# Two tiles and GpSimd's DMA queue for side loads, c broadcast by TensorE, and half of a projection in unsplit fp32

## The chip, the cores and the metric

The kernel runs on one core of a Trainium2 chip. The metric is the time of one execution on the device in microseconds; lower is better. TensorE (PE) multiplies matrices out of SBUF into PSUM, VectorE (DVE) and ScalarE (ACT) work element by element, SyncE (SP) issues DMAs here, and GpSimd (POOL) is nearly idle.

## The reference

A decoder trunk of two layers over 256 tokens of width 1024, in fp32. Each layer has a token mixer (layer 0: a short gated convolution; layer 1: differential attention) and then a PEER expert mixer. Each of the four sub-layers takes shift, scale and gate from a vector c:

```python
m = silu(c) @ ada_w[i, s] + ada_b[i, s]         # 1024 x 3072: shift, scale - 1, gate - 1
h = x * (1 + scale) + shift
f = mixer(h)
x = layer_norm(ALPHA * x + (1 + gate) * f, ln_g[i, s], ln_b[i, s])

# the conv mixer
gb, gc, xv = split(h @ w_in, 3); y = gb * conv3(gc * xv); f = y @ w_out
# PEER: the 16 best of 128 x 128 product keys for each of 8 heads and each token
f = sum over the chosen experts of softmax(score) * gelu(h . u[expert]) * v[expert]
```

## The kernel before

**Precision.** A product of fp32 operands is made of three products of split operands. `split` (L92) makes a high part by an ACT copy (L87) and a low part by a DVE subtraction (L90); `mm3` (L140 to L143) and its copies in `project_out` (L352) and `V_steps` (L874) add high x high, high x low and low x high. Small products of attention (L517, L551) and transposes (L207) use fp32 as it is.

**Tiles.** Weights come in tiles of 128 x 1024 fp32, 512 KB, by SP's queue. `raw` (L76) hands out such tiles from a ring of 6 (`STREAM`), in turn with a second ring while a token mixer has one (12 in conv, 4 in attention). `spt` (L80) hands out split tiles from a ring of 10 (`SPBUFS`). In the conv mixer SP issues in program order (`Sync`, L65); after it the scheduler sets the order.

**Order.** Each mixer yields steps, each with a first half (load and split) and a second half (multiply), and `pipeline` (L104) runs the first halves three steps ahead of the second. The framework's scheduler then fixes the order on each engine from its own estimate of times; each engine works through its queue in that order and waits where something is missing.

**The ada columns.** shift, scale and gate are sums over rows of `ada_w` times silu(c). One column (`ada_column`, L173) is one 512 KB load and one DVE pass with accumulation against `csb`, silu(c) on all partitions (L177). There are 96: 16 set the first h of the conv mixer (`h_first`, `h_second`), 24 more fill the conv mixer, 48 the first expert layer and 8 the second. These fills are generators (`ada_unit`, L179: eight columns, two for each `yield`, and a sum) that `advance` (L324) moves on between steps; in the projection of the conv mixer they are held behind the last y (`behind`, L227).

**The conv mixer** (L358). x comes as one DMA of 1 MB behind the first four ada columns. h is made by four pairs of columns of x; `half_second` multiplies the first half of `conv_w_in` as h comes, `project_step` (L305) the second half; `use` (L364) makes y, split into `yh` and `yl`; `project_out` (L338) multiplies by `conv_w_out` in four steps q of two rows of weights k.

**Norm** (L235). Behind each mixer: gate times the accumulators (L266), plus ALPHA times X (L268), square sums on ACT (L270), scaling (L286), then transposes and splits of the next h (`make_hT`, L200). ln's gain and bias are put on X later (`affine`, L292, its DVE passes in L297), out of the way.

**The expert layer** (L646). The query products, then `topk`, then three chunks of the 128 rows of keys (46, 42, 40): U products with Gelu into a ring, gate matrices (`G_step`: DVE makes one-hot factors in L825 to L829, PE multiplies them in L838, DVE multiplies the ring in L840), V products (L874). U of the third chunk and V of the first alternate; V of the third chunk, `vs(2)`, comes last and needs all gates of its chunk.

Of the kernel before, what the change touches and what calls it, by code (L numbers as in the profile page):

```python
# [11 lines left out]
F32 = mybir.dt.float32  # L12
# [16 lines left out]
PH = 8  # L29
# [8 lines left out]
SPBUFS = 10  # L38
STREAM = 6
# [4 lines left out]
def tile_trunk(ctx: ExitStack, tc: tile.TileContext, x, c, columns, ada_w, ln_g, ln_b, conv_w_in_a, conv_w_in_b,  # L44
# [103 lines left out]
    nc.sync.dma_start(csb, rows_bcast(c[0], D))  # L148
    X = const.tile([P, NT, D], F32, name="X")

# [14 lines left out]
    act.activation(csb, csb, AF.Silu)  # L165
# [7 lines left out]
    def ada_column(i, s, part, n, dst):  # L173

        w = raw()
        sync.dma_start(w, ada_w[i, s, part, n])
        return lambda: dve.scalar_tensor_tensor(w, w, 1.0, csb, op0=ALU.mult, op1=ALU.mult, accum_out=dst)  # L177

    def ada_unit(i, s, part):  # L179
        a = small.tile([P, KC], F32, tag="ada", name="ada", bufs=2)  # L180
        for q in range(KC // 2):
            for f in [ada_column(i, s, part, n, a[:, n:n + 1]) for n in (2 * q, 2 * q + 1)]:
                f()
            yield
        at = slice(None), 2 * i + s, slice(KC * part, KC * part + KC)
        dve.tensor_tensor(mod[at], a, ada_bT[at], op=ALU.add)
        yield
# [47 lines left out]
    class Norm:  # L235
# [102 lines left out]
    def project_out(w, yT, accs, engs):  # L338
        def first(q):
            return [load(w[(2 * q + kk) * P:(2 * q + kk + 1) * P, :], engs[kk]) for kk in range(2)]  # L340

        def second(q, parts):
            if q == 0:
                accs.extend(new_accs())
            yh, yl = yT[q]
            for t in range(NT):
                rows = slice(t * P, (t + 1) * P)
                for kk, (wh, wl) in enumerate(parts):
                    k = 2 * q + kk
                    for lhs, rhs, first, last in ((yh, wh, True, False), (yh, wl, False, False), (yl, wh, False, True)):  # L350
# [7 lines left out]
    def conv_mixer(j, hT, cp, fill, prep):  # L358
        gbT = [None] * KC
        gcT = [None] * KC  # L360
        yh = cp.tile([P, KC, T], F32R, name="yh")
        yl = cp.tile([P, KC, T], F32R, name="yl")

        def use(n, ps):  # L364
# [9 lines left out]
            y = cp.tile([P, T], F32, tag="y", name="y", bufs=2)  # L374
# [642 lines left out]
```

## Time and profile before

| what | value |
|---|---|
| median of 3 runs | 1955.66 us (1955.38 to 1959.54) |
| profiled execution | 1956.54 us, its span 1954.8 us |
| PE busy | 1885.1 us, 96% of the span |
| DVE busy | 1550.6 us, 79% |
| ACT busy | 905.3 us, 46% |
| POOL busy | 9.5 us |
| data moved | 378.87 MB, mean 194 GB/s |

The span is that of the instructions on the core, 1.7 us less than the execution. Busy time of PE is the time in which some matmul was under way, also where it ran at a lower clock. A chain of waits on a page names what released each instruction; the views below give the instructions themselves.

### The profile page before, as it was taken

The page shows a single profiled execution, that of the slowest core. Times are in us where ns is not written, and L with a number is a line of the kernel's source. Part 1 is how long each engine was busy: PE and PEld are TensorE (multiplying, and loading weights), DVE is VectorE, ACT ScalarE, POOL GpSimd, SP SyncE. Part 2 cuts the span into 40 slices and gives each one's busy share as a digit, 9 for nine tenths or more (in the row PEclk, how much of TensorE's full clock was granted, in tenths as well). Part 3 has the DMA queues.
Part 4 walks back from the last instruction along what each step waited for, and adds up shares of the span by engine and source line. Part 5 has one row for each costly group of instructions (what it writes and reads, how often), then busy time and mean ns, then how long its engine had stood idle before and what let it go on. Part 6 is the DMA issues. An engine that isn't in the chain of part 4 may idle for free.

```text
span 1954.8 us, 36946 instructions
## 1 busy us (share of the span) xinstructions
PE 1885.1 (96%) x14858; PEld 1720.6 (88%) x14858; DVE 1550.6 (79%) x3138; ACT 905.3 (46%) x1191; POOL 9.5 (0%) x28
## 2 busy tenths in 40 slices
PE   7969999999999999989899899999999999999897
PEld 6969999999999988867798799999999999888786
DVE  7989887887888888876677788878878766888755
ACT  4534555334444444434466545653444444444443
POOL 0000000000000000000100000000000000000000
PEclk9989999999999999999999999999999999999999
DMA  9955655556778765568753246555567555555563
GB/s 383 366 187 159 185 180 177 163 158 210 249 243 256 232 201 173 173 198 279 241 182 111 86 152 184 183 174 161 161 208 226 173 175 181 168 169 181 173 194 97
DMA packets 104412, 378.87 MB, mean 194 GB/s; under 512 B 11568, under 2 KB 12208, under 8 KB 104240
## 3 DMA queue, kind: packets, MB, share of 16 engines
q1 hardware_dynamic: 104096, 376.42, 59.8%
q8 instruction: 116, 1.90, 0.4%
q14 instruction: 56, 0.46, 0.1%
q10 hardware_dynamic: 144, 0.09, 0.0%
HBM read 375.42 MB, written 1.05 MB: 193 GB/s over the span
## 4 chain that ended last, share of the span: by engine, by line
PE 91%; DVE 5%; DMA 2%; issue 1%; ACT 1%; SPq 0%; DVEq 0%; ACTq 0%
PE acc L874 34%; PE ps L141 15%; PE ps L142 15%; PE ps L143 15%; PE ps L838 4%; DVE raw L177 2%; PE acc L352 2%; PE acc L142 2%; PE acc L141 2%; PE acc L143 2%; DVE spt L90 1%; DMA raw<-in_ada_w 1%; DMA X<-in_x 1%; PE ps L517 0%; DMA gsub<-in_attn_subln_g 0%
## 5 line engine op out<-in xcount | busy, mean ns | idle before, releaser
L87 ACT ACTIVATE spt<-raw 128x1024 fp32r<-128x1024 f32 x608 | 641.1, 1058 | 745.3 <-PE ps L142 416.5
L90 DVE TENSOR_TENSOR spt<-raw,spt 128x1024 fp32r<-128x1024 f32 x608 | 741.0, 1222 | 171.3 <-ACT spt L87 166.5
L141 PE MATMUL ps<-hh,spt 128*128 128x256 f32 x2400 | 684.9, 286 | 2.9 <-DVE hh L214 2.4
L142 PE MATMUL ps<-hl,spt 128*128 128x256 f32 x2400 | 681.0, 284 | 0.6 <-DVE hl L90 0.6
L143 PE MATMUL ps<-hh,spt 128*128 128x256 f32 x2400 | 680.5, 284 | 0.0
L874 PE MATMUL acc<-spt,wh 128*128 128x512 f32 x2048 | 565.9, 396 | 4.4 <-ACT wh L87 4.4
L141 PEld LDWEIGHTS ps<-hh,spt 128*128 128x128 f32 x2400 | 460.6, 192 | 6.8 <-issue 3.0
L142 PEld LDWEIGHTS ps<-hl,spt 128*128 128x128 f32 x2400 | 461.4, 192 | 4.0 <-DVE hl L90 0.9
L143 PEld LDWEIGHTS ps<-hh,spt 128*128 128x128 f32 x2400 | 461.3, 192 | 0.0
L874 PEld LDWEIGHTS acc<-spt,wh 128*128 128x128 f32 x2048 | 375.9, 188 | 75.8 <-ACT wh L87 4.6
L874 PE MATMUL acc<-spt,wl 128*128 128x512 f32 x1024 | 319.6, 392 | 3.6 <-DVE wl L90 3.6
L874 PEld LDWEIGHTS acc<-spt,wl 128*128 128x128 f32 x1024 | 191.9, 188 | 44.8 <-DVE wl L90 5.1
L177 DVE SCALAR_TENSOR_TENSOR raw<-raw,csb 128x1024 f32<-128x1024 f32 x96 | 116.1, 1223 | 57.8 <-DMA raw<-in_ada_w 57.7
L87 ACT ACTIVATE wh<-ring 128x512 fp32r<-128x512 f32 x128 | 79.9, 627 | 159.0 <-PE acc L874 148.9
L840 DVE SCALAR_TENSOR_TENSOR ring<-ps,ring 128x368 f32<-128x368 f32 (+2 forms) x192 | 98.1, 512 | 68.6 <-PE ps L838 68.0
L825 DVE TENSOR_TENSOR A<-iota_e,jT 128x1024 f16<-128x1024 f16 x192 | 131.0, 683 | 0.0
L829 DVE TENSOR_TENSOR B<-B,gT 128x368 f16<-128x368 f16 (+2 forms) x384 | 125.1, 334 | 4.0
L90 DVE TENSOR_TENSOR wl<-ring,wh 128x512 fp32r<-128x512 f32 x128 | 88.0, 689 | 38.7 <-ACT wh L87 38.2
L838 PEld LDWEIGHTS <-A 128*128 128x128 f16 x3072 | 91.0, 96 | 31.1 <-issue 14.3
L838 PE MATMUL ps<-B,A 128*128 128x46 f16 (+2 forms) x3072 | 111.7, 182 | 6.6 <-DVE B L829 6.6
L805 ACT ACTIVATE ring<-ps 128x512 f32<-128x512 f32 x128 | 74.7, 584 | 33.8 <-PE ps L143 33.7
L827 DVE TENSOR_TENSOR B<-iota_e,iT 128x368 f16<-128x368 f16 (+2 forms) x192 | 63.4, 331 | 0.0
(204 smaller groups left out, 1179.9 us busy)
## 6 DMA issues: line engine op xcount, KB each, us to landing
raw<-in_peer_u SPq DMA_DIRECT2D x256, 512.0 KB, 3.8
raw<-in_peer_v SPq DMA_DIRECT2D x256, 512.0 KB, 3.9
raw<-in_ada_w SPq DMA_DIRECT2D x96, 512.0 KB, 4.7
raw<-in_peer_w_q SPq DMA_DIRECT2D x32, 512.0 KB, 4.1
raw<-in_attn_w_qk SPq DMA_DIRECT2D x16, 512.0 KB, 4.4
raw<-in_conv_w_in_a SPq DMA_DIRECT2D x12, 512.0 KB, 10.2
raw<-in_conv_w_in_b SPq DMA_DIRECT2D x12, 512.0 KB, 10.2
raw<-in_conv_w_out SPq DMA_DIRECT2D x8, 512.0 KB, 7.2
```

Source lines behind the costliest of these rows:

```text
L87: act.activation(o, i, AF.Copy, scale=scale)
L90: return eng.tensor_tensor(o, a, b, op=ALU.subtract)
L141: pe.matmul(ps, ah, bh, start=first, stop=False)
L142: pe.matmul(ps, ah, bl, start=False, stop=False)
L143: pe.matmul(ps, al, bh, start=False, stop=last)
L177: return lambda: dve.scalar_tensor_tensor(w, w, 1.0, csb, op0=ALU.mult, op1=ALU.mult, accum_out=dst)
L805: act.activation(ring[:, s:s + 2, :].rearrange("p j t -> p (j t)"), st["ps"], AF.Gelu)
L825: dve.tensor_tensor(by_two(A), numbers(0, KEYS), pairs(jT, KEYS), op=ALU.is_equal)
L829: dve.tensor_tensor(by_two(B[:, h]), by_two(B[:, 1]), pairs(gT[:, h], n), op=ALU.mult)
L838: pe.matmul(ps[:, t, :], A[:, t, :], B[:, h, t, :], start=h == 0, stop=h == 1)
L840: dve.scalar_tensor_tensor(r, ps.rearrange("p t j -> p j t"), 1.0 / GSCALE, r, op0=ALU.mult, op1=ALU.mult)
L874: pe.matmul(acc[t][hf], lhs[:, jj, rows], rhs[:, hf * 512:(hf + 1) * 512], start=first and jp == 0 and jj == 0, stop=last and last_pair an ...
```

## The change

- **Start.** c comes as one row of 4 KB on ACT's queue. TensorE multiplies it by a row of ones, two fp32 products of 512 columns, and ACT takes Silu from PSUM into `csb`. x comes in four quarters of 256 columns, the first on ACT's queue at the start, the others on SP's with the ada columns of their pair.
- **Side loads.** Two tiles of their own (`side`) and GpSimd's queue serve the 48 and 8 ada columns of the expert layers and the gain and bias rows of `affine` there. `ada_units` loads one column ahead and moves on one column for each `yield`. `STREAM` goes from 6 to 5, `SPBUFS` from 10 to 9.
- **Places.** conv: 2 columns for each of six groups of steps and 4 behind each projection step, in place of 2 and up to 4. Expert layers: a column in two of three steps; `affine` moves from step 6 of `vs(2)` to the steps 30, 33 and 35.
- **Projection.** The rows k = 4 to 7 of `conv_w_out` and of y are not split: one fp32 product in place of three.
- **topk** takes its scratch from unused rows of the ring in place of four split tiles.

```diff
-SPBUFS = 10
-STREAM = 6
+SPBUFS = 9
+STREAM = 5
...
     csb = const.tile([P, D], F32, name="csb")
-    nc.sync.dma_start(csb, rows_bcast(c[0], D))
+    crow = raw()[0:1, :]
+    act.dma_start(crow, c)
     X = const.tile([P, NT, D], F32, name="X")
+    def load_x(q):
+        cols = slice(q * 256, (q + 1) * 256)
+        (sync if q else act).dma_start(X[:, :, cols], x[0][:, cols].rearrange("(t p) d -> p t d", p=P))
+    load_x(0)
...
-    act.activation(csb, csb, AF.Silu)
+    ones = wk.tile([1, P], F32, tag="B", name="ones")
+    pool.memset(ones, 1.0)
+    for hf in range(2):
+        ps, cols = bank(), slice(hf * 512, (hf + 1) * 512)
+        pe.matmul(ps, ones, crow[:, cols], start=True, stop=True)
+        act.activation(csb[:, cols], ps, AF.Silu)
...
-    def ada_column(i, s, part, n, dst):
-        w = raw()
-        sync.dma_start(w, ada_w[i, s, part, n])
+    def side():
+        return stream.tile([P, D], F32, tag="side", name="side", bufs=2)
+    def ada_column(i, s, part, n, dst, tile=raw):
+        w = tile()
+        (sync if tile is raw else pool).dma_start(w, ada_w[i, s, part, n])
         return lambda: dve.scalar_tensor_tensor(w, w, 1.0, csb, op0=ALU.mult, op1=ALU.mult, accum_out=dst)
-    def ada_unit(i, s, part):
-        a = small.tile([P, KC], F32, tag="ada", name="ada", bufs=2)
-        for q in range(KC // 2):
-            for f in [ada_column(i, s, part, n, a[:, n:n + 1]) for n in (2 * q, 2 * q + 1)]:
-                f()
-            yield
...
+    def ada_units(*which, tile=raw):
+        def compute(at, a, f, final):
+            f()
+            if final:
+                dve.tensor_tensor(mod[at], a, ada_bT[at], op=ALU.add)
+        loaded = None
+        for i, s, part in which:
...
+            for n in range(KC):
+                f = ada_column(i, s, part, n, a[:, n:n + 1], tile)
+                if loaded:
+                    compute(*loaded)
+                    yield
+                loaded = at, a, f, n == KC - 1
+        compute(*loaded)
         yield
...
-    def ln_params(i, s):
-        gb = raw(), raw()
-        sync.dma_start(gb[0], rows_bcast(ln_g[i, s], D))
-        sync.dma_start(gb[1], rows_bcast(ln_b[i, s], D))
+    def ln_params(i, s, tile=raw):
+        gb = tile(), tile()
+        queue = sync if tile is raw else pool
+        queue.dma_start(gb[0], rows_bcast(ln_g[i, s], D))
+        queue.dma_start(gb[1], rows_bcast(ln_b[i, s], D))
...
-        def affine(self, _):
-            gb = ln_params(self.i, self.s)
+        def affine(self, tile=raw):
+            gb = ln_params(self.i, self.s, tile)
+            yield
             for t in range(NT):
                 for n, op in enumerate((ALU.mult, ALU.add)):
                     dve.tensor_tensor(X[:, t, :], X[:, t, :], gb[n], op=op)
+                yield
...
-    def project_out(w, yT, accs, engs):
+    def project_out(w, yT, accs, engs, whole=KC):
         def first(q):
...
+                if q >= whole:
+                    parts.append((raw(),))
+                    sync.dma_start(parts[-1][0], rows)
+                else:
+                    parts.append(load(rows, engs[kk]))
...
+                    if q >= whole:
+                        products = (yT[q][0], ws[0], True, True),
+                    else:
+                        (yh, yl), (wh, wl) = yT[q], ws
+                        products = (yh, wh, True, False), (yh, wl, False, False), (yl, wh, False, True)
...
-            dve.tensor_tensor(y, y, gbT[k], op=ALU.mult)
+            last["y"] = dve.tensor_tensor(y, y, gbT[k], op=ALU.mult)
+            if k >= half:
+                return
             copy(yh[:, k, :], y)
-            last["y"] = sub(dve, yl[:, k, :], y, yh[:, k, :].bitcast(F32))
+            sub(dve, yl[:, k, :], y, yh[:, k, :].bitcast(F32))
...
-            if q == 0:
-                sync.dma_start(X, x[0].rearrange("(t p) d -> p t d", p=P))
+            if q:
+                load_x(q)
...
-                    yield advance(fill)
+                    yield advance(fill, 2)
...
-            for st in project_out(conv_w_out[j], yT, acc, SUBS):
+            for st in project_out(conv_w_out[j], yT, acc, SUBS, 2):
                 yield st
-                yield advance(fill, 2, ("hT", "y"))
+                yield advance(fill, 4, ("hT", "y"))
...
-                    yield None, late
+                    yield drain(late())
...
+        cand = scratch(PH * NCAND).rearrange("p (h k) -> p h k", **hk)
+        f = scratch(6 * P).rearrange("p (n k) -> p n k", n=6)
+        eq, keys = (scratch(1024).bitcast(F16).rearrange("p (h k a) -> p h k a", h=PH, k=TOPK) for _ in range(2))
...
-                if n % 2 == 1:
+                if n % 3 != 0:
                     yield advance(fill)
...
+            rest = late(side)
             for n, v in enumerate(vs(2)):
                 yield v
-                if n % 3 == 2:
+                if n % 3 != 0 and n < n2 - 10:
                     yield advance(fill)
-                if n == 6:
-                    yield None, late
+                if n == n2 - 10:
+                    yield drain(fill)
+                    yield advance(rest)
                 if n == n2 - 8:
-                    yield drain(fill)
                     yield None, prep
+                if n in (n2 - 7, n2 - 5):
+                    yield advance(rest)
...
-        fill = units((0, 0, 2), (0, 1, 0), (0, 1, 1))
+        fill = ada_units((0, 0, 2), (0, 1, 0), (0, 1, 1))
...
-    fill = units((0, 1, 2), (1, 0, 0), (1, 0, 1), (1, 0, 2), (1, 1, 0), (1, 1, 1))
+    fill = ada_units((0, 1, 2), (1, 0, 0), (1, 0, 1), (1, 0, 2), (1, 1, 0), (1, 1, 1), tile=side)
...
-        acc = peer(1, hT, pp, units((1, 1, 2)), norm.prepare, late)
+        acc = peer(1, hT, pp, ada_units((1, 1, 2), tile=side), norm.prepare, late)
```

## Rows read from the trace of the kernel before

**Rows 1.** Page, busy tenths of TensorE in 40 slices of the span
```profile
PE   7969999999999999989899899999999999999897
```

**Rows 2.** Table by stretches: engines' busy us (instructions), PEclk, DMA share, GB/s
```profile
60.00:80.00 20.00, 20.00 (x169) 20.00 (x168) 19.99 (x36) 10.20 (x18) 0.40 (x4) 1.00 1.03 408
...
455.00:701.00 246.00, 246.00 (x1987) 225.14 (x1986) 201.90 (x328) 107.62 (x123) 0.00 (x0) 1.00 0.76 244
...
1435.00:1680.00 245.00, 245.00 (x1979) 224.15 (x1977) 177.63 (x274) 106.91 (x123) 0.00 (x0) 1.00 0.62 194
```

**Rows 3.** In order of time to 17 us: start, duration, engine, line, operation
```profile
2.04 1.86 PE L415 MATMUL acc<-iota_a,zero 128*128 128x512 f16 x4 [2.04 <-POOL z L372]
...
6.96 1.23 DVE L177 SCALAR_TENSOR_TENSOR raw<-raw,csb 128x1024 f32<-128x1024 f32 x1 [1.07 <-DMA raw<-in_ada_w]
...
13.30 1.97 PE L207 MATMUL ps<-ident,X 128*128 128x128 f32 x8 [9.39 <-DMA X<-in_x]
14.46 1.02 ACT L213 ACTIVATE h<-ps,mod 128x256 f32<-128x256 f32 x2 [6.36 <-PE ps L207]
...
16.99 0.39 PE L422 MATMUL acc<-hh,spt 128*128 128x256 f32 x1 [0.24 <-ACT hh L87]
```

**Rows 4.** The same view, TensorE, from the conv mixer into the first expert layer
```profile
113.44 0.62 PE L352 MATMUL acc<-spt,yl 128*128 128x512 f32 x2
...
132.58 0.77 PE L141 MATMUL ps<-hh,spt 128*128 128x256 f32 x2 [1.35 <-DVE hh L214]
```

**Rows 5.** The same view, TensorE, from attention into the second expert layer
```profile
1099.98 0.63 PE L352 MATMUL acc<-spt,yl 128*128 128x512 f32 x2
...
1110.09 0.36 PE L141 MATMUL ps<-hh,spt 128*128 128x256 f32 x1 [1.05 <-DVE hh L214]
```

**Rows 6.** The same view, VectorE, 102 to 123 us
```profile
102.18 1.22 DVE L90 TENSOR_TENSOR spt<-raw,spt 128x1024 fp32r<-128x1024 f32 x1 [0.62 <-ACT spt L87]
103.33 0.75 DVE L90 TENSOR_TENSOR yl<-y,yh 128x256 fp32r<-128x256 f32 x2
104.00 1.22 DVE L177 SCALAR_TENSOR_TENSOR raw<-raw,csb 128x1024 f32<-128x1024 f32 x1
...
122.50 1.23 DVE L268 SCALAR_TENSOR_TENSOR spt<-X,spt 128x1024 f32<-128x1024 f32 x1
```

**Rows 7.** The same view, all engines, end of the first layer's gates
```profile
847.81 0.61 PE L874 MATMUL acc<-spt,wl 128*128 128x512 f32 x2
...
856.03 1.23 DVE L177 SCALAR_TENSOR_TENSOR raw<-raw,csb 128x1024 f32<-128x1024 f32 x1 [0.93 <-DMA raw<-in_ada_w]
...
858.84 3.25 PE L874 MATMUL acc<-spt,wh 128*128 128x512 f32 x8 [3.03 <-ACT wh L87]
```

**Rows 8.** The same view, TensorE, end of the second layer's gates
```profile
1826.83 0.61 PE L874 MATMUL acc<-spt,wl 128*128 128x512 f32 x2
...
1833.27 2.11 PE L874 MATMUL acc<-spt,wh 128*128 128x512 f32 x8 [1.32 <-ACT wh L87]
1836.57 0.73 PE L874 MATMUL acc<-spt,wl 128*128 128x512 f32 x2 [1.20 <-DVE wl L90]
```

**Rows 9.** The same view, TensorE, last V product of each expert layer
```profile
972.25 0.39 PE L874 MATMUL acc<-spt,wl 128*128 128x512 f32 x1
...
1943.49 0.39 PE L874 MATMUL acc<-spt,wl 128*128 128x512 f32 x1
```

**Rows 10.** Who waited for whom, 860 to 960 us: total us, times, longest
```profile
DVE raw L177 <- DMA raw<-in_ada_w: 18.9, 8, 3.5
```

**Rows 11.** DMA issues: destination, source, queue, count, KB each, median us to landing
```profile
raw<-in_ada_w SPq DMA_DIRECT2D x96, 512.0 KB, 4.7
...
out_x<-spt SPq DMA_DIRECT2D x4, 256.0 KB, 2.1
```

**Rows 12.** The same view, TensorE: split and fp32 products
```profile
99.97 1.09 PE L352 MATMUL acc<-spt,yh 128*128 128x512 f32 x4
...
1022.09 1.05 PE L551 MATMUL ps<-v,aT 128*128 128x128 f32 x8
```

More of the change, by code (lines that the diff above doesn't have):

```diff
@@ L171, in tile_trunk @@
     mod = const.tile([P, 4, 24], F32, name="mod")
-    def ada_column(i, s, part, n, dst):
-        w = raw()
-        sync.dma_start(w, ada_w[i, s, part, n])
-        return lambda: dve.scalar_tensor_tensor(w, w, 1.0, csb, op0=ALU.mult, op1=ALU.mult, accum_out=dst)
-    def ada_unit(i, s, part):
-        a = small.tile([P, KC], F32, tag="ada", name="ada", bufs=2)
-        for q in range(KC // 2):
-            for f in [ada_column(i, s, part, n, a[:, n:n + 1]) for n in (2 * q, 2 * q + 1)]:
-                f()
-            yield
-        at = slice(None), 2 * i + s, slice(KC * part, KC * part + KC)
-        dve.tensor_tensor(mod[at], a, ada_bT[at], op=ALU.add)
+    def side():
[3 more added lines that the diff above has]
+        (sync if tile is raw else pool).dma_start(w, ada_w[i, s, part, n])
+        return lambda: dve.scalar_tensor_tensor(w, w, 1.0, csb, op0=ALU.mult, op1=ALU.mult, accum_out=dst)
+    def ada_units(*which, tile=raw):
[5 more added lines that the diff above has]
+        for i, s, part in which:
+            a = small.tile([P, KC], F32, tag="ada", name="ada", bufs=3)
+            at = slice(None), 2 * i + s, slice(KC * part, KC * part + KC)
+            for n in range(KC):
[5 more added lines that the diff above has]
+        compute(*loaded)
         yield
@@ L336, in drain @@
         return None, second
-    def project_out(w, yT, accs, engs):
+    def project_out(w, yT, accs, engs, whole=KC):
         def first(q):
-            return [load(w[(2 * q + kk) * P:(2 * q + kk + 1) * P, :], engs[kk]) for kk in range(2)]
+            parts = []
+            for kk in range(2):
+                rows = w[(2 * q + kk) * P:(2 * q + kk + 1) * P, :]
+                if q >= whole:
[3 more added lines that the diff above has]
+                    parts.append(load(rows, engs[kk]))
+            return parts
         def second(q, parts):
@@ L344, in second @@
                 accs.extend(new_accs())
-            yh, yl = yT[q]
             for t in range(NT):
                 rows = slice(t * P, (t + 1) * P)
-                for kk, (wh, wl) in enumerate(parts):
+                for kk, ws in enumerate(parts):
                     k = 2 * q + kk
-                    for lhs, rhs, first, last in ((yh, wh, True, False), (yh, wl, False, False), (yl, wh, False, True)):
+                    if q >= whole:
[3 more added lines that the diff above has]
+                        products = (yh, wh, True, False), (yh, wl, False, False), (yl, wh, False, True)
+                    for lhs, rhs, first, last in products:
                         for hf in range(2):
@@ L360, in conv_mixer @@
         gcT = [None] * KC
-        yh = cp.tile([P, KC, T], F32R, name="yh")
-        yl = cp.tile([P, KC, T], F32R, name="yl")
+        yh = cp.tile([P, KC // 2, T], F32R, name="yh")
+        yl = cp.tile([P, KC // 2, T], F32R, name="yl")
+        yf = cp.tile([P, KC // 2, T], F32, name="yf")
         def use(n, ps):
@@ L373, in use @@
             dve.tensor_tensor(z[:, 2:], ps, gcT[k], op=ALU.mult)
-            y = cp.tile([P, T], F32, tag="y", name="y", bufs=2)
+            half = KC // 2
+            y = yf[:, k - half, :] if k >= half else cp.tile([P, T], F32, tag="y", name="y", bufs=2)
             col = lambda w: smT[:, 160 + 8 * w + k:161 + 8 * w + k]
@@ L445, in steps @@
                         yield project_step(conv_w_in_b[j, m, 2 * n + b - 4], blk, hT, use, bank, SUBS[b])
[L446 removed]
+                    yield advance(fill, 2)
             yield None, prep
[L448 to L449 removed]
+            yT = [(yh[:, 2 * q:2 * q + 2], yl[:, 2 * q:2 * q + 2]) for q in range(2)]
+            yT += [(yf[:, 2 * q:2 * q + 2],) for q in range(2)]
+            for st in project_out(conv_w_out[j], yT, acc, SUBS, 2):
                 yield st
[L451 removed]
+                yield advance(fill, 4, ("hT", "y"))
             yield drain(fill, ("hT", "y"))
@@ L716, in topk @@
             s0, s1 = sv4[:, :, 0, :], sv4[:, :, 1, :]
-            cand = sp.tile([P, PH, NCAND], F32, tag="sp", name="cand")
             dve.tensor_tensor(cand[:, :, 0:16], s0[:, :, 0:1].to_broadcast([P, PH, 16]), s1, op=ALU.add)
@@ L739, in topk @@
             yield
-            f = sp.tile([P, 6, P], F32, tag="sp", name="f")
             pos = po.rearrange("t h k -> t (h k)")
```

7 lines of the change are left out of this document (removed).

## The prediction

> **What bounds the kernel now.** I first read the page's slices [rows 1]: TensorE (PE) is at nine tenths or more nearly everywhere. So time can only be won where PE stands still, or by giving it less to multiply. The table by stretches [rows 2] says the same by stage: in 60 to 80 us PE is busy for all 20.00 us, VectorE (DVE) for 19.99, the granted clock is 1.00, and the DMA engines move 408 GB/s at a share of 1.03; in the stretches 455 to 701 and 1435 to 1680 us, the same program part of the first and second expert layer, PE is busy for every microsecond of 246 and 245, though the first holds 32 columns of ada weights and the second 8. Work that is taken off DVE, or off the SP queue, in such stretches is worth nothing.
>
> The PE holes, then. (a) The start: the first real matmul begins at 16.99, behind x, for which PE's transposes wait until 13.30 [rows 3]. (b) From the conv mixer to the first expert layer: PE ends its output projection at 114.06 (113.44 + 0.62) and begins the next at 132.58, 18.5 us later [rows 4]. The same passage from attention to the second expert layer runs from 1100.61 to 1110.09, 9.5 us [rows 5]. The difference is DVE: it does 14 ada columns between 104.00 and 122.50, one row like the other, and the norm's L268 begins only then [rows 6]. (c) In the first expert layer, where the last gates meet the last V chunk, PE multiplies no V from 848.42 to 858.84, 10.4 us; in the second layer the same place runs from 1827.44 to 1833.27, 5.8 us, with a last hole of 1.20 at 1836.57 [rows 7, 8]. (d) Behind (c) more is lost in the first layer: from the end of the row at 847.81 to the end of its V products at 972.64 it takes 124.2 us, in the second layer 1827.44 to 1943.88, 116.4 [rows 7, 8, 9]. That is 7.8 us for one and the same work. What differs is 16 ada columns on DVE, for whose transfers DVE waited 18.9 us in 860 to 960 [rows 10], and the clock: eight like matmuls took 3.25 us at 858.84 and 2.11 at 1833.27 [rows 7, 8].
>
> **The change, part by part.** The profiled execution took 1956.54 us around a span of 1954.8, 0.9 above the median of the three timed runs; I sum against 1956.54.
>
> **Start.** c's 512 KB broadcast goes, which at 408 GB/s [rows 2] is 1.28 us of every later landing in a stretch where the DMA engines are full. x comes by quarters; the first goes ahead of the ada tiles, so the first ada sum waits for 0.26 MB (0.64 us) more and the first h for 0.79 MB (1.9 us) less. c now costs PE two fp32 products of 512 columns. Four f16 products of 512 columns took 1.86 us at this early point, 0.43 apart [rows 3]; an fp32 product runs as two records, each twice as long (below), so some 1.7 us each, 3.5 in all. The row of c is 4 KB on ACT's queue, and nothing in the trace is that small; the quickest row is the output's 2.1 us to landing [rows 11]. Issued near 0.7, with 2.1, 3.5 for the products and half of the Silu behind them, csb is ready near 6.9, where the first ada column starts today (6.96, [rows 3]). The fourth column ends at about 6.96 + 4 x 1.23 = 11.9 as today, but h no longer waits for x and its transposes at 13.30: the first h comes near 12 instead of 14.46 [rows 3]. The bounds: 0.5 us, if c's row needs as long as a full tile does here, and 3.5, if the ada tiles come 1.28 sooner and csb with them. I take 2.0, since PE and DVE are both nearly full afterwards and must carry it on.
>
> **Half of the output projection in fp32.** For four of eight rows of weights DVE loses a subtraction of 1.22 us and one of y of 0.38 (two took 0.75, [rows 6]), ACT two copies. PE loses 12 products a row and gets 4 in fp32. Four split products of 512 columns take 1.09 us; without the tail of the last (one alone lasts 0.39, [rows 9]) that is (1.09 - 0.39) / 3 = 0.23 each. Eight records of fp32 with 128 columns take 1.05 [rows 12]; the code has one product there to two records. With a tail of 0.28, estimated from the 0.39 less 0.11, a record takes (1.05 - 0.28) / 7 = 0.11, so a product 0.22 for 128 columns and 0.88 for 512. Per row 4 x 0.88 = 3.5 against 12 x 0.23 = 2.8; over four rows PE gets 3.0 us longer. It is back to back from 91.5 to 114, so all of this is on the path: 3.0 us lost (from 0, if records of 512 columns pipeline better, to 5).
>
> **The fill of the conv mixer.** One column per step and two or four steps at a time: 12 columns instead of 10 come before the projection, 12 instead of 14 behind the last y. At 1.22 us a column [rows 6], 12 columns are 14.6 us. The last y comes earlier by what DVE lost, 4 x (1.22 + 0.38) less the 2 columns moved ahead (2.4), 4.0 us, and by 2.0 from the start: columns from about 98.0 to 112.6. PE ends at 114.06 - 2.0 + 3.0 = 115.1. So PE sets the end again, by 2.5 us, and the norm starts as in attention; PE goes on 9.5 later, at 124.6 instead of 132.58. Gain of start, projection and fill together: 8.0. If the time of DVE's lost subtractions only turns into waits for PE, the columns run from 104.0 - 2.0 + 2.4 = 104.4 to 119.0, and PE waits 3.9 us for them. The four raw tiles of unsplit weights stay held until PE has used them, and loads of later columns queue behind them on SP in program order, ahead of the next layer's first weights; that is R1.
>
> **Own tiles and the GpSimd queue.** 48 columns and the gain and bias rows of the layer norm leave the SP queue and its tiles and are loaded one column ahead. In 455 to 701 this is worth nothing (246 against 245). At (c) and (d) the waits of DVE for transfers go. The floor there is the second layer's 116.4, itself 1.2 shorter when L297, which sits ahead of its last hole, moves behind step 33. What stays is DVE's time for the columns, some still in the chain: DVE did the one at 856.03 right before the hole ended [rows 7]; one or two of 1.23 us. First layer: 7.8 + 1.2 - 2.5 = 6.5; second: 1.0. The Trainium skill ("DMA: Bandwidth & Descriptors", Issuing engines are not separate DMA queues) says that the queue of another engine saves only the time of issuing, since all run on the same 16 DMA engines. By that rule this part would be worth 0 and the result R2's; no run here shows it yet. GpSimd's own queue holds nothing else in these stretches (9.5 us of work in the whole span), so a column waits there only for its tile.
>
> **Smaller tile rings** (5 raw, 9 split) and topk's scratch in the ring: 8 split tiles are three steps ahead and the one in work; ACT and DVE wait for PE in these stretches, not PE for them. 0 here, up to 2 lost in attention.
>
> Sum: 8.0 + 6.5 + 1.0 = 15.5, so 1956.5 - 15.5 = 1941.0, and 1940 against the median.
>
> **The rivals.** R1: the fill still ends last in the conv mixer, because its loads queue behind held tiles or DVE's order puts columns ahead of the norm. Against it the 14 columns ran without one wait for a transfer [rows 6]; for it the margin of 2.5 us is thin. The passage then stays, and what is left is 1956.5 - 2.0 + 3.0 - 7.5 = 1950.0, about 1949 against the median. R2: the expert layers gain nothing, DVE waiting for transfers of the one queue as for the other; 1956.5 - 8 = 1948.5, about 1948. R3, slower: transfers from GpSimd land so late that DVE, which takes its work in order, becomes the bound. In 455 to 701 DVE is idle for 246 - 201.9 = 44 us, with 26 columns after the change: 1.7 us of wait each are free. Two advances lie 246 / 40 = 6.1 us apart or more, and two tiles let one transfer run ahead, so it decides from a landing of 7.8 us; SP's ada tiles land in 4.7 (the median, [rows 11]). At 8.8 us each column costs 1.0 us, 26 in all, and the result is 1941 + 26, about 1966. The Trainium skill ("SBUF — State Buffer", Who interferes with whom) speaks for such a thing: GpSimd writes the descriptors of its DMAs itself and is shut out while DVE runs in a two-port mode. It also says that tensor_tensor has no such mode, and that is most of what DVE runs here; no run here shows either. R4, the change doesn't do what it says: columns stand in the chain at both places as before. Then start and L297 give 2.0 + 2 x 1.2 and fp32 takes 3.0: 1955.1, about 1954.
>
> **How the numbers follow.** Forecast 0.62, R1 0.11, R2 0.12, R3 0.08, R4 0.07. The predicted time is 1940, with a range of its own from 1932 (start 3.5, fp32 0, no column left in the chain: 7 less) to 1946 (columns ending 3.9 late, fp32 5). R1, R2 and R4 lie up to 1954; R3 and what is under 1931 are left out. A measurement of this kernel can tell about 0.2%, 4 us: faster is under 1951.7. Faster 0.82 (forecast, most of R1 and R2), same 0.10 (R4, rests), slower 0.08 (R3).
>
> **What would show it.** Start: first L422 near 14.5, and ada's first column near 6.9. Conv: no column between the last y's and the norm that ends after PE; 9.5 us from PE's projection to the next layer's first product instead of 18.5. fp32: 32 records of some 0.43 us. Expert layers: waits of DVE for ada transfers gone from 840 to 960, the first layer's stretch from the last gates to the end near 118 instead of 124.2. I am wrong if GpSimd's tiles land in over 7 us, if the norm waits for a column, or if new PE holes stand in 140 to 830, where there is none now.

## The result: 3.6% slower, and the profile after

The changed kernel takes 2028.08 us (2025.46 to 2029.76, 4 runs), the kernel before 1957.20 (1955.38 to 1959.54, 4 runs) on the same chip: a ratio of 1.036, 95% interval 1.0341 to 1.0379. The forecast was 1940, with a range up to 1954. The profiled execution took 2026.64 us with a span of 2024.9, against 1956.54 and 1954.8.

The page of the changed kernel, busy times and tenths in 40 slices of about 50 us (PEld is PE's loading of weights, PEclk the granted clock):

```profile
PE 1923.2 (95%) x14846; PEld 1735.2 (86%) x14846; DVE 1546.6 (76%) x3130; ACT 902.6 (45%) x1184; POOL 41.5 (2%) x89
PE   7989939999999999999998799899999999999997
DVE  6989999887766678865576699958877667788655
PEclk9989969999999999999999799999999999999999
```

PE has a slice of 3 tenths near 250 to 300 us, where there was none before [rows 1], and the granted clock falls in the same slice. DVE is at nine tenths there. PE is also busy for 38 us more in all (1923.2 against 1885.1) with almost the same products, so not all of the loss is waiting.

The stages, from the first or last row of a kind in the timeline of PE (starts, us; line numbers of the changed kernel are higher: V products L922 for L874, projections L395 for L352, c's product L177, an ada column L194 for L177):

| stretch | before | after | difference |
|---|---|---|---|
| start to the first query product of the first expert layer | 132.58 | 129.95 | -2.6 |
| from there to its first V product | 328.35 | 366.86 | +38.5 |
| first to last V product | 511.32 | 510.29 | -1.0 |
| to the first product of the attention projection | 94.07 | 91.50 | -2.6 |
| that projection, to the start of its last product | 33.90 | 51.60 | +17.7 |
| to the second layer's first V product | 339.74 | 353.28 | +13.5 |
| first to last V product | 503.53 | 510.35 | +6.8 |
| to the end | 11.27 | 11.04 | -0.2 |

The sum is +70.1, the difference of the spans. Timeline rows at some of these boundaries, of before and then of after, and the three longest waits of PE in the stretches that grew (start, length, instruction, count, idle time before it):

```profile
460.93 1.09 PE L874 MATMUL acc<-spt,wh 128*128 128x512 f32 x4
1439.95 1.09 PE L874 MATMUL acc<-spt,wh 128*128 128x512 f32 x4
```

```profile
129.95 0.77 PE L141 MATMUL ps<-hh,spt 128*128 128x256 f32 x2 [1.55 <-DVE hh L241]
292.99 0.45 PE L825 MATMUL ps<-ident,ring 128*128 128x128 f32 x1 [30.68 <-DVE ring L822]
496.81 1.08 PE L922 MATMUL acc<-spt,wh 128*128 128x512 f32 x4
1098.60 1.10 PE L395 MATMUL acc<-spt,yh 128*128 128x512 f32 x4
1113.54 1.08 PE L589 MATMUL ps<-ident,s 128*128 128x128 f32 x4 [5.74 <-DVE s L587]
1299.44 0.45 PE L825 MATMUL ps<-ident,ring 128*128 128x128 f32 x1 [5.33 <-DVE ring L822]
```

PE waits 30.68 us for topk in the first layer and 5.33 in the second, and 5.74 in attention. What fills DVE ahead of the first wait is seen when the 48 side columns are looked up by their line, in the changed kernel (count, shortest/median/longest ns, first and last start; then who waited for them, us and times):

```profile
L194 DVE SCALAR_TENSOR_TENSOR side<-side,csb x48: 1197/1214/1226, 133.8 to 343.0; 128x1024 f32<-128x1024 f32 x48
  POOL side L193: 139.2, 23
```

All 48 run from 133.8 to 343.0 us, beside the query products and topk; in the kernel before they begin behind the first V product, at 461. GpSimd waits for DVE to give tiles back (139.2 us in 23 waits); its transfers land in 4.8 us, the median of all 56 (first line below), and DVE waits 6.2 us in all for the 48. Below that, the stretch from the first query product to the first product of the gates, in the changed kernel and then in the kernel before (length, then busy time and count of PE, PEld, DVE, ACT, POOL; clock, DMA share, GB/s):

```profile
side<-in_ada_w POOLq DMA_DIRECT2D x56, 512.0 KB, 4.8
130.00:361.00 231.00, 197.82 (x1609) 196.82 (x1610) 219.76 (x659) 103.71 (x131) 26.40 (x50) 0.92 0.76 257
```

```profile
133.00:326.00 193.00, 193.00 (x1606) 192.83 (x1606) 161.88 (x548) 102.74 (x131) 0.00 (x0) 0.99 0.56 174
```

DVE's work in this stretch was 161.88 us under 193.00 of PE; 48 columns of 1.21 us add 58, which makes 219.9 (measured 219.76). DVE has become the bound of the stretch.

### The profile page after: what moved, and what is told of

It is laid out like the page before. It is cut to its first block, busy times and chain, and to the rows that moved or that the text cites. A ratio compares the mean times of both kernels' runs of the same rounds, so it can differ in the third digit from the quotient of the medians.

```text
span 2024.9 us, 37081 instructions
## 1 busy us (share of the span) xinstructions
PE 1923.2 (95%) x14846; PEld 1735.2 (86%) x14846; DVE 1546.6 (76%) x3130; ACT 902.6 (45%) x1184; POOL 41.5 (2%) x89
## 4 chain that ended last, share of the span: by engine, by line
PE 87%; DVE 6%; issue 3%; DMA 2%; ACT 2%; POOL 0%; DVEq 0%; SPq 0%; POOLq 0%; ACTq 0%
PE acc L922 35%; PE ps L141 13%; PE ps L142 13%; PE ps L143 13%; PE ps L886 4%; PE acc L395 2%; DVE spt L90 2%; PE acc L143 1%; PE acc L141 1%; PE acc L142 1%; DMA side<-in_ada_w 1%; DMA raw<-in_ada_w 1%; DVE side L194 1%; PE acc L470 0%; ACT spt L87 0%
## 5 line engine op out<-in xcount | busy, mean ns | idle before, releaser
L922 PE MATMUL acc<-spt,wh 128*128 128x512 f32 x2048 | 570.4, 399 | 2.5 <-ACT wh L87 2.5
L922 PEld LDWEIGHTS acc<-spt,wh 128*128 128x128 f32 x2048 | 376.4, 188 | 82.1 <-ACT wh L87 2.7
L922 PE MATMUL acc<-spt,wl 128*128 128x512 f32 x1024 | 324.5, 397 | 0.0
L922 PEld LDWEIGHTS acc<-spt,wl 128*128 128x128 f32 x1024 | 191.6, 188 | 43.3
L886 PE MATMUL ps<-B,A 128*128 128x46 f16 (+2 forms) x3072 | 116.4, 182 | 5.7 <-DVE B L877 5.7
L888 DVE SCALAR_TENSOR_TENSOR ring<-ps,ring 128x368 f32<-128x368 f32 (+2 forms) x192 | 97.2, 506 | 17.7 <-PE ps L886 17.7
L194 DVE SCALAR_TENSOR_TENSOR side<-side,csb 128x1024 f32<-128x1024 f32 x56 | 67.7, 1213 | 10.2 <-DMA side<-in_ada_w 10.1
```

Source lines behind the costliest of these rows:

```text
L886: pe.matmul(ps[:, t, :], A[:, t, :], B[:, h, t, :], start=h == 0, stop=h == 1)
L888: dve.scalar_tensor_tensor(r, ps.rearrange("p t j -> p j t"), 1.0 / GSCALE, r, op0=ALU.mult, op1=ALU.mult)
L922: pe.matmul(acc[t][hf], lhs[:, jj, rows], rhs[:, hf * 512:(hf + 1) * 512], start=first and jp == 0 and jj == 0, stop=last and last_pair an ...
```

## The experiments

Three theories for the 70 us: (T1) the columns, pulled forward by the scheduler; (T2) the smaller rings; (T3) V products that are slower by themselves (they start 232 ns apart instead of 227 to 228, in every stretch). The parts of the change that were meant to gain were then measured one at a time. Times of the kernel before are medians of 13 or 14 runs on the same chip as the variant's. They are 1958.15 to 1959.23, and 1957.20 beside the changed kernel, so a difference between variants of two chips is good to some 2 us.

**Columns held.** In the changed kernel, at every place where the expert layers move `fill` or `rest` on (one is shown):

```diff
-        sub(eng, lo, src, hi.bitcast(F32))
+        last["lo"] = sub(eng, lo, src, hi.bitcast(F32))
...
-                    yield advance(fill)
+                    yield advance(fill, 1, ("hT", "lo"))
```

> The changed kernel, with one thing added: every ada column and every pass of the gain and bias rows in the expert layers is queued on DVE behind the latest subtraction of a weight split at its place in the program, so that the scheduler can't pull it forward. Theory (columns pulled into the query products and topk, where DVE has no time to spare): the PE hole of 30.7 us at 262 to 293 us goes, the stretch from the first query product to the first V product of the first expert layer falls from 366.9 to about 328 us, and the time from 2028 to about 1990; in the second layer up to 13 more go. Rival (topk's single scratch in the ring, or the smaller rings, make that hole): the hole stays and the time stays above 2015.

Measured: 1975.28 us against 1959.23 before (ratio 1.0077, 1.006 to 1.0094), 52.8 less than the changed kernel. The held variant's columns by their line, and its stretch of the query products:

```profile
L194 DVE SCALAR_TENSOR_TENSOR side<-side,csb x48: 1215/1219/1226, 472.5 to 951.3; 128x1024 f32<-128x1024 f32 x48
```

```profile
130.00:324.00 194.00, 193.60 (x1609) 193.47 (x1610) 161.08 (x548) 103.77 (x132) 0.00 (x0) 0.99 0.57 173
```

The hole is gone, DVE has 161.08 us of work again, and the first layer takes 329.5 us to its first V product. In the second layer the same stretch takes 329.6 instead of 343.4, so its 13.5 us were the 8 columns too, not topk's single scratch, which this variant still has. T1 stands.

**Ones moved.** The new row of ones took the first place in a pool and moved the tiles behind it by 2944 bytes. In the changed kernel:

```diff
-    ones = wk.tile([1, P], F32, tag="B", name="ones")
+    ones = wk.tile([P, 2, T], F32, tag="wh", name="ones")[0:1, 0, 0:P]
```

> The changed kernel, with the row of ones in the first tile of another tag of the same pool, one that held the first place before; so the tiles of the V products' stationary operand stand at the addresses of the kernel before. Order and count of instructions are those of the changed kernel. Theory (addresses in SBUF make the V products of 512 columns slower, 232 ns from start to start in place of 227): the interval goes back to 227, which over 3072 products is 15 to 17 us, so the time falls from 2028 to about 2012. Rival (what slows them is GpSimd's transfers or DVE beside them): the interval stays at 232 and the time within 4 us of 2028.

Measured: 2012.14 us (ratio 1.0266, 1.0249 to 1.0283), 15.9 less. V products alone in 80 us near the end of the second layer: the changed kernel, the variant, the kernel before (length, PE busy and count, PEld, clock, DMA).

```profile
1930.00:2010.00 80.00, 80.00 (x346) 64.88 (x345) 1.00 0.51 164
```

```profile
1910.00:1990.00 80.00, 80.00 (x354) 66.25 (x353) 1.00 0.60 189
```

```profile
1860.00:1940.00 80.00, 80.00 (x355) 66.24 (x354) 1.00 0.52 158
```

346 products against 354, PE full and the clock at 1.00 in each: 80 / 346 - 80 / 354 = 5.2 ns each, 16 us over 3072. The instructions and their order are the same; only addresses differ. So T3 stands, and addresses are its cause.

**64 bytes.** In the kernel before, one pad each: ahead of the pool of the V products' stationary operand, or at the end of the constants, so that weights and operand both move.

```diff
+    wk.tile([P, 16], F32, tag="pad", name="pad", bufs=1)
```

```diff
+    const.tile([P, 16], F32, name="pad")
```

> The kernel before with 64 bytes of nothing on each partition ahead of the pool that holds the stationary operand of the V products; order and instructions stay. That operand then starts at 113504 in place of 113440, the weights it meets stay at 56096 and every 4096 behind. Theory (a V product is fast only where the two operands start at the same place in a 512-byte row: 288 and 288 before, 160 and 288 in the changed kernel): now 352 and 288, interval 232 ns in place of 227.6, 1959 + 15, about 1974. Rival (only the changed kernel's address is bad): 227.6 ns and 1959.

> The kernel before with 64 bytes of nothing at the end of the constants, so that weights, h and the stationary operand of the V products all move by 64 bytes: weights at 56160 (352 in a 512-byte row), the operand at 113504 (352 as well). Theory (what counts is where one operand stands against the other): 227.6 ns and about 1959. Rival (what counts is where the stationary operand stands by itself, 352 being slow with the weights at 288): 233 ns and about 1971.

Measured, with the pad ahead of the pool: 1970.81 us (one run). With both moved: 1957.82 (one run). The rows in the same order:

```profile
1860.00:1940.00 80.00, 80.00 (x344) 64.11 (x343) 1.00 0.60 185
```

```profile
1860.00:1940.00 80.00, 80.00 (x354) 66.25 (x353) 1.00 0.52 160
```

Where the first tile of each operand starts in the built programs, in bytes within a partition (in brackets the remainder by 512; the further tiles lie multiples of 2048 bytes behind it):

| kernel | weights start at | stationary operand at | V products in 80 us |
|---|---|---|---|
| before | 56096 (288) | 113440 (288) | 355 |
| changed | 60192 (288) | 116384 (160) | 346 |
| ones moved | 60192 (288) | 113440 (288) | 354 |
| pad ahead of the operand | 56096 (288) | 113504 (352) | 344 |
| pad ahead of both | 56160 (352) | 113504 (352) | 354 |

288 with 288 and 352 with 352 are fast, 160 or 352 with 288 are slow. So what counts here is where one operand stands against the other: remainders 64 and 128 bytes apart are slow, equal ones fast. The two times are single runs; the reading rests on the counts. What the period is, and why this costs time, no run shows.

**Rings alone.** In the kernel before:

```diff
-SPBUFS = 10
-STREAM = 6
+SPBUFS = 9
+STREAM = 5
```

with topk's scratch in the ring as in the changed kernel.

> The kernel before, with only the smaller rings (5 raw tiles, 9 split tiles) and topk's scratch in the ring. Theory (nine split tiles are too few for the attention projection, whose steps take four): the projection from its first to its last product takes about 51 us in place of 33.9, and the time is 1957 + 18, about 1975; if topk's one scratch also holds up the second expert layer, up to 1985. The prediction: 0 to 2 us, 1957 to 1959. Rival (the own tiles or the queue of GpSimd upset attention): 1957, the projection at 33.9 us.

Measured: 1969.15 us against 1959.23 (ratio 1.0051, 1.0034 to 1.0067). The same holes in the attention projection as in the changed kernel, in this variant:

```profile
1063.05 1.09 PE L352 MATMUL acc<-spt,yh 128*128 128x512 f32 x4
1077.97 1.09 PE L541 MATMUL ps<-ident,s 128*128 128x128 f32 x4 [5.74 <-DVE s L539]
1096.37 0.73 PE L352 MATMUL acc<-spt,yl 128*128 128x512 f32 x2 [1.23 <-DVE yl L90]
1104.56 0.50 PE L572 MATMUL ps<-ident,o 128*128 128x128 f32 x2 [1.64 <-DVE o L570]
1113.02 0.63 PE L352 MATMUL acc<-spt,yl 128*128 128x512 f32 x2
```

The projection takes 50.2 us where it took 33.9; it starts 4.6 us earlier behind the first expert layer (80.3 us in place of 84.9), and the rest of the 16.3 is lost. The second expert layer comes to its first V product in 328.5 us: topk's scratch costs nothing.

**Five raw tiles, ten split tiles.** In the variant above, with nothing else changed:

```diff
-SPBUFS = 9
+SPBUFS = 10
```

> The kernel before with 5 raw tiles in place of 6 and topk's scratch in the ring, and ten split tiles as before. With these and nine split tiles the attention projection took 50.2 us from first to last product and the kernel 10 us more than before. Theory (nine split tiles are the cause): 33.9 us again and a time within 2 us of 1959. Rival (the raw tiles are): about 50 us and 1969.

Measured: 1956.61 us against 1958.27 (ratio 0.9993, 0.9983 to 1.0002), the projection from 1068.87 to 1102.75, 33.9 us. So T2 stands for the split tiles alone: nine in place of ten cost 1969.15 - 1956.61 = 12.5 us (11.4 by the ratios).

**Front alone.** In the kernel before, only the start, the conv mixer's fill and the half fp32 projection, with the ones where nothing moves.

```diff
+    crow = raw()[0:1, :]
+    act.dma_start(crow, c)
...
-                    yield advance(fill)
+                    yield advance(fill, 2)
...
-            for st in project_out(conv_w_out[j], yT, acc, SUBS):
+            for st in project_out(conv_w_out[j], yT, acc, SUBS, 2):
```

> The kernel before, with only the start, the fill of the conv mixer and the half fp32 projection of the change; the row of ones stands where no other tile of the pool moves. Rings, topk and the expert layers are those of before. The prediction: 8 us less, about 1949. Theory from the trace of the changed kernel, where the start brought nothing and the stretch up to the next layer's first product 2.6 us: 1954 to 1955. Rival (side columns of the expert layer, fetched by GpSimd in the first microseconds, spoiled the start of the changed kernel): 1951 or less, the first product of the conv mixer near 15 us.

Measured: 1955.08 us against 1959.23 (ratio 0.998, 0.9971 to 0.999): 4.2 gained, as the theory from the trace said, half of the prediction's 8. The rival falls: without side columns in the first microseconds the first product comes at 18.64, later than in either kernel. Its fp32 products, and the passage to the expert layer:

```profile
104.53 13.89 PE L406 MATMUL acc<-raw,yf 128*128 128x512 f32 x32
124.18 3.65 PE L248 MATMUL ps<-ident,X 128*128 128x128 f32 x16 [5.76 <-DVE gbc L299]
129.39 0.77 PE L141 MATMUL ps<-hh,spt 128*128 128x256 f32 x2 [1.56 <-DVE hh L255]
```

**Three repairs.** In the changed kernel: columns held, ones moved, and

```diff
-SPBUFS = 9
-STREAM = 5
+SPBUFS = 10
+STREAM = 4
```

> The changed kernel with three repairs at once: columns held in their place on DVE as in the held variant, the row of ones where no other tile moves, and ten split tiles again, paid for with a raw tile (4 in place of 5); the two own tiles and GpSimd's queue stay. Theory (pulled columns, addresses and split tiles are all of the loss): 1975.3 of the held variant less 16 for the addresses and 11 for the attention projection (45.2 us there from first to last product, 33.9 before), so about 1948, and its projection in attention takes 34 us. Rival (the raw tiles are what the attention projection lacks): with 4 of them that projection stays at 45 or more and the time at 1959 or above.

Measured: 1949.75 us against 1958.27 (ratio 0.9958, 0.9942 to 0.9975), the projection of attention 33.9 us. The theory's 1948 is just inside the runs (1947.99 to 1951.41), and four raw tiles do the attention projection no harm.

**Common ring.** As three repairs, with 6 raw tiles and no own ones:

```diff
-        return stream.tile([P, D], F32, tag="side", name="side", bufs=2)
+        return raw()
```

> As the variant with three repairs, but the side loads take their tiles from the common ring, which has 6 tiles as in the kernel before; GpSimd's queue, the loading one column ahead and the places stay. The prediction put 6.5 us in the first expert layer and 1.0 in the second down to own tiles and the queue together. Theory (the queue and the places do it): first to last V product of the first expert layer in about 505 us, in place of 511.3, and the time within 3 us of the variant with own tiles. Rival (own tiles do it): 511, and 5 to 7 us more than that variant.

Measured: 1946.92 us against 1958.27 (ratio 0.9944, 0.9928 to 0.9961). First to last V product of the first layer 505.4 us (455.47 to 960.91), as with own tiles (505.5). The own tiles are worth nothing that shows.

**SP's queue.** As the common ring, with SP issuing the side loads (the gain and bias rows too, not shown):

```diff
-        (sync if tile is raw else pool).dma_start(w, ada_w[i, s, part, n])
+        sync.dma_start(w, ada_w[i, s, part, n])
```

> As the variant with the common ring of 6 tiles, but SP's queue issues the side loads too; GpSimd's issues none. Places and the loading ahead stay. The prediction gave own tiles and GpSimd's queue 7.5 us together, and the variant showed that the own tiles are not needed for it. Theory A (the queue does it: on SP a side load waits behind others and others behind it): first to last V product of the first expert layer 509 to 511 us in place of 505.4, time 1951 or more. Theory B (the places and the loading ahead do it, the queue only saves its own issue): 505 to 506 us, 1947 within 3.

Measured: 1945.74 us against 1958.15 (ratio 0.993, 0.9913 to 0.9948). Its first and last V product of the first layer, and the holes where the last gates come:

```profile
458.42 1.09 PE L922 MATMUL acc<-spt,wh 128*128 128x512 f32 x4
847.19 0.19 PE L886 MATMUL ps<-B,A 128*128 128x40 f16 x1 [1.27 <-DVE B L877]
849.70 0.19 PE L886 MATMUL ps<-B,A 128*128 128x40 f16 x1 [2.32 <-DVE B L877]
853.14 2.07 PE L922 MATMUL acc<-spt,wh 128*128 128x512 f32 x4 [1.30 <-ACT wh L87]
963.88 0.39 PE L922 MATMUL acc<-spt,wl 128*128 128x512 f32 x1
```

505.5 us again: theory B. The queue is worth nothing either. What is left, by elimination, is where the columns stand, held there and loaded one ahead; no run separates these three. With all columns ahead of this stretch (ones moved) it took 504.6 us, so little more was to be won in it. That the queue is worth nothing agrees with the rule of the Trainium skill ("DMA: Bandwidth & Descriptors", Issuing engines are not separate DMA queues) that another engine's queue saves only the time of issuing. This variant and the common ring are faster than both kernels, with intervals clear of them.

**Mended start.** As the common ring, with two things reordered:

```diff
-    load_x(0)
     smT = const.tile([P, 184], F32, name="smT")
     act.dma_start(smT, columns)
+    load_x(0)
...
+            if q == 0 and m < 2:
+                with behind("mod"):
+                    parts = [p.rearrange("p (k n) -> p k n", k=2) for p in split(parts, SUBS[m % 2])]
```

> As the variant with the common ring of 6 tiles (1946.9), with the start mended in two places: the columns of biases go ahead of the first quarter of x on ACT's queue (DVE's first operation waits for them), and the first two weights are split on DVE behind the sum of the first four ada columns, not ahead of it (two passes of 1.2 us stand there). Theory (the start gave nothing because of these two): the first product of the conv mixer at 15 to 15.5 us in place of 18.3, and since PE is full from there to the end of the projection, 2.5 to 3 us off the whole, 1944. Rival (the ada tiles land too late, at 8.1 and 9.8 us, to let more be won): 17 us or later, 1946.

Measured: 1950.37 us against 1958.15 (ratio 0.9961, 0.9947 to 0.9975), no better than the common ring. Rows of its start:

```profile
13.00 0.16 DVE L448 TENSOR_TENSOR mod<-ah,smT 128x4 f32<-128x4 f32 x1
14.31 0.63 ACT L87 ACTIVATE hh<-h 128x512 fp32r<-128x512 f32 x1
19.93 1.05 ACT L87 ACTIVATE spt<-raw 128x1024 fp32r<-128x1024 f32 x1
21.03 0.58 PE L475 MATMUL ps<-hh,spt 128*128 128x256 f32 x1 [1.25 <-ACT spt L87]
```

The sum and h came as early as the theory said, but with the DVE half of the split also its ACT half moved back, to 19.93, and PE waited for that until 21.03. The edit did not test the theory cleanly, and neither forecast came true; what an early h is worth stays open.

**All split.** As the mended start, with no fp32 in the projection:

```diff
-            for st in project_out(conv_w_out[j], yT, acc, SUBS, 2):
+            for st in project_out(conv_w_out[j], yT, acc, SUBS):
```

> As the variant with the mended start, but all rows of the output projection of the conv mixer are split again (three products, none in fp32). The prediction charged the fp32 half with 3.0 us on PE and credited it with 6.4 us of DVE. Theory (PE bounds the conv mixer now): 48 products of 0.23 us in place of 16 of 0.87, so PE ends 2.8 us earlier and the whole is 2 to 3 us shorter than that variant. Rival (DVE bounds the end, with columns behind the last y): the norm waits for columns again, and the whole is 2 to 5 us longer.

Measured: 1955.76 us against 1958.15 (ratio 0.9989, 0.9979 to 0.9998), 5.4 more than the mended start. PE ends the projection at 117.3 in place of 119.6, and then waits for DVE:

```profile
122.11 1.22 DVE L193 SCALAR_TENSOR_TENSOR raw<-raw,csb 128x1024 f32<-128x1024 f32 x1
124.45 1.21 DVE L193 SCALAR_TENSOR_TENSOR raw<-raw,csb 128x1024 f32<-128x1024 f32 x1
131.79 3.61 PE L233 MATMUL ps<-ident,X 128*128 128x128 f32 x16 [14.46 <-DVE X L313]
```

The rival stands, at a little more than its 2 to 5 us: the columns run among the norm's passes, until 125.6. The fp32 half costs PE 2.9 us (13.89 less 48 x 0.23) and gains more than that back.

## Why the prediction was wrong, step by step

- **"Smaller tile rings: 0, up to 2 lost in attention"** failed: 12.5 us, from the split tiles. The reasoning looked at the expert layers, where a step takes two split tiles; a step of the projection takes four, and in attention it stands between steps of other kinds.
- **"In 455 to 701 this is worth nothing"** rested on the columns staying there. That was the large error: 52.8 us. In the kernel before, nothing in the code held a column's DVE pass but the order in which it got a tile of the common ring; with tiles and a queue of its own each was ready early, and the scheduler put it where DVE had no room. That the columns came early and what it cost is measured; that the tiles or the queue let them go, and not the new places, is argued from the code, since no run has the common ring without the hold. I had the number that decides it: 161.88 us of DVE work beside 193.00 of PE leaves 31 us, and 48 columns want 58. The prediction named new PE holes in 140 to 830 as a sign that it was wrong, and the 30.68 us are there, but it had no mechanism for them. R3 had the right direction, to 1966 and with a chance of 0.08, by another mechanism: transfers that land late (it decided from 7.8 us; the median was 4.8).
- **Not in the sum at all:** the addresses, 15.9 us.
- **Start, 2.0 gained:** 0, the first product at 16.98 as before. The rows of the changed kernel:

```profile
3.85 3.78 PE L177 MATMUL ps<-raw,ones 1*128 1x512 f32 x4
8.30 1.23 DVE L194 SCALAR_TENSOR_TENSOR raw<-raw,csb 128x1024 f32<-128x1024 f32 x1 [8.30 <-ACT csb L178]
13.10 0.16 DVE L449 TENSOR_TENSOR mod<-ah,smT 128x4 f32<-128x4 f32 x1
13.49 1.06 ACT L87 ACTIVATE spt<-raw 128x1024 fp32r<-128x1024 f32 x1 [3.71 <-DMA raw<-in_conv_w_in_a]
14.45 1.00 ACT L240 ACTIVATE h<-ps,mod 128x256 f32<-128x256 f32 x2
15.35 1.05 ACT L87 ACTIVATE spt<-raw 128x1024 fp32r<-128x1024 f32 x1
16.30 0.62 ACT L87 ACTIVATE hh<-h 128x512 fp32r<-128x512 f32 x1
16.98 1.22 PE L469 MATMUL acc<-hh,spt 128*128 128x256 f32 x4 [7.72 <-ACT hh L87]
```

  c's products took 3.78 us (3.5 forecast), but the first ada column began at 8.30, not 6.9: the products wait until 3.85 behind the zeroing products of 2.06, and the second half of the Silu comes behind the last of them. Then two copies of weights stand in ACT's order, one ahead of h and one ahead of hh, 2.1 us. The prediction counted neither order. Nor did it count that, with x's first quarter transposed by 9.26, PE stands idle ahead of its first product and runs the next ones at half pace (the last section).
- **fp32, 3.0 lost:** right. 32 records in 13.89 us are 0.87 per product (0.88 forecast), 13.9 - 48 x 0.23 = 2.9 us.
- **Fill, net 8.0 gained with start and projection:** 4.2 in the variant with the front alone, 2.6 in the changed kernel's trace. The columns behind the last y run from 99.69 to 111.22 (98.0 to 112.6 forecast; the last one and the next pass of DVE stand below), and DVE then waits for PE, so PE does set the end:

```profile
110.08 1.22 DVE L194 SCALAR_TENSOR_TENSOR raw<-raw,csb 128x1024 f32<-128x1024 f32 x1
114.74 0.69 DVE L294 TENSOR_TENSOR spt<-acc,rows 128x512 f32<-128x512 f32 x1 [3.44 <-PE acc L395]
```

  But PE ends at 118.99, not 115.1: 2.0 for the start that wasn't won, the rest for the slow first products (below). And the passage is 11.0 us, not 9.5: two columns still stand between the norm's passes, at 116.21 and 118.49.
- **Own tiles and queue, 6.5 and 1.0 gained:** the first layer's size was about right, the cause wrong. With columns held and addresses restored, the V stretches take 505.5 and 502.0 us in place of 511.3 and 503.5 (SP's queue): 5.9 and 1.5. Neither the tiles nor the queue is needed for it. The 1.5 of the second layer isn't shown to be the change's at all: five raw tiles and ten split tiles, with the expert layers' columns as in the kernel before, take 502.0 us there, and the pad ahead of both, with all instructions as before, 505.5. From the end of the V products ahead of the last gates (847.19 - 1.27 = 845.92) to the end at 964.27 it is 118.4 us; the forecast was 118, before it was 124.2.

The three losses together, 52.8 + 15.9 + 12.5 = 81.2, are what lies between the changed kernel (2028.08) and the common ring (1946.92). That they meet it to 0.1 us is luck, since the runs are of several chips: by the ratios to the kernel before, the three are 55, 18 and 11 us, some 84 in all, against 82. The 11.3 us that this stands below the kernel before are the front (4.2) and the V stretches (5.9, and 1.5 of open cause), within the 2 us.

A slip in the prediction's sum changes none of this: its lower bound, 7 under 1940, is 1933, not 1932.

## What to carry to other kernels

A shared ring of tiles can also be an order (here read off the code): before work gets buffers and a queue of its own, ask what else holds it in its place, compare its time with the room that its engine has in the stretch where it could go, and write the order out. Size a ring by the step that takes the most of it, not by the stage that runs longest. After adding any tile, look at the addresses of the operands of the most frequent product.

## What the runs showed of the hardware

- A product of fp32r with 128 x 512 columns took 5.2 ns more of some 226 when the start addresses of its operands left different remainders by 512 (table above), with PE full and the clock at 1.00. The attention projection's products, with operands at 320 and 288, are such a case in the kernel before: 232 ns.
- Products behind an idle stretch ran at half the pace, in a stretch for which the profile prints a clock of 1.00 (the last number but two of a line) because it has no record of the clock there. The changed kernel by stretch and in three rows of the timeline, then the kernel before by stretch:

```profile
21.00:24.00 3.00, 3.00 (x16) 1.00 1.02 408
```

```profile
19.47 0.41 PE L473 MATMUL acc<-hh,spt 128*128 128x256 f32 x1
19.68 0.41 PE L469 MATMUL acc<-hh,spt 128*128 128x256 f32 x1
19.89 0.41 PE L470 MATMUL acc<-hl,spt 128*128 128x256 f32 x1
```

```profile
21.00:24.00 3.00, 3.00 (x27) 1.00 1.03 411
```

  The products start 0.21 us apart in the changed kernel and, in the kernel before, 0.11 (3.00 / 27): 256 columns in 0.21 us are 1.2 in a nanosecond, the lower of the clock's two levels, 1.2 and 2.4 GHz. The trace's first record of the granted clock begins at 23.81 us in the changed kernel, at full clock, and from 23.89 on its products start 0.12 us apart; in the kernel before it begins at 16.39. So the clock's record and the pace agree, and the view counts the time ahead of the first record as full clock. In the changed kernel PE had stood idle from 9.26 to 16.98; in the kernel before it did transposes from 13.30 up to the first real product [rows 3]. The first record begins between 21.7 and 26.0 in all nine kernels with the new start, and between 16.1 and 22.9 in the five with the old one, so the rise comes later with the new start on the whole, by an amount that differs from run to run. In these two traces it is 27 products against 51 begun by 24 us; the kernel before then waits for the next part of h, and the last of the 576 products of h with the mixer's first weights starts 2.3 us later in the changed kernel (92.91 against 90.61), though the first starts at the same time.
